# A fixed order at the head of a decoder layer, wider root tiles and other k-cuts of its input projection

## The chip, the cores and the metric

The kernel runs on one core of a Trainium2 chip. The metric is the device time of one execution in microseconds (us). Before the change it is 1656.35 us, the median of three runs (1655.63 to 1658.23). Five engines of the core work side by side, each on its own queue of instructions: TensorE (PE, matmuls; its weight loads are a row of their own, PEld), VectorE (DVE), ScalarE (ACT), GpSimd (POOL) and SyncE (SP), which here only issues DMAs.

## What is computed

One inference step of a decoder layer, for 256 new prompt tokens and 8 x 4 sample tokens, so 288 token columns (T) of 2048 features, and 9 conditioning vectors (one of the prompt, eight of the samples). In short:

```
mod  = silu(c) @ w_ada + b_ada                    # 6 x 2048 values for each vector
h    = rms(x, g_mix) * (1 + sc_m) + sh_m          # D_MODEL = 2048
proj = h @ w_in                                   # 9216 columns = 72 tiles of 128
b_gate, c_gate, hc, u, v, ga, gb = split(proj)
ya   = b_gate * shortconv(c_gate * hc);  yb = gelu(u) * spatial_gate(rms(gelu(v), g_v))
x   += gt_m * ((sigmoid(ga) * (ya @ w_pa) + sigmoid(gb) * (yb @ w_pb)) @ w_out)
h2   = rms(x, g_ffn) * (1 + sc_f) + sh_f
x   += gt_f * ((silu(gate) * up) @ w_ffn_out),   gate, up = split(h2 @ w_ffn_in)
```

The outputs are the final normalised x of both groups, the convolution states and the normalised v rows.

## The kernel before, in words

**Products.** Features lie on the partitions, tokens on the columns. Every weight matrix is streamed from memory in blocks into a ring of five raw buffers (`RAW`, 128 x 2048 float32, 1 MB, each). A block is used in pieces of at most four 128 x 128 tiles (`SEG`): ScalarE casts the piece to a rounded part `hi` (L364), VectorE subtracts it from the raw weights to get `lo` (L366); rings of four pieces each (`SPB`) hold the results. Activations are split alike. TensorE then does three matmuls of 288 columns for each weight tile: hi by hi (L380), hi by lo (L381), lo by hi (L382), into one of four PSUM banks named `pm`.

**The k-cuts of w_in.** `STREAMS` cuts the 16 feature tiles (k) of `h @ w_in`: `wA` takes k = 0 for all 72 output tiles, 8 output tiles a block (9 blocks); `wB` takes k = 1 and 2, 8 tiles a block (9 blocks); `wC` k = 3 to 7, 3 tiles a block (24 blocks); `wD` k = 8 to 15. After each pass of an output tile a "sink" moves its PSUM bank into a partial sum in SBUF: `sinkA` copies (odd tiles on ScalarE, L510, even ones on VectorE, L512), `sinkB` and `sinkC` add on VectorE (L517, L520, L523).

**The root.** The mean square of x is not known when wA begins. For the first `RAWX` = 40 tiles, wA therefore multiplies x times its gain without the root, with ten extra columns (298 in all) that carry the shift; `rescale` on GpSimd later multiplies each such partial sum by the root `rb` (L483) and adds a shift to the sample columns (L484). The squares of x are made by ScalarE and GpSimd, `sums1` adds them on TensorE, `rstd1` and `norm1` make `rb`. `mk_h1(k)` makes the normalised, modulated and split feature tile k (VectorE L203, ScalarE L233 and L239, GpSimd L236 and L237, VectorE L244).

**Modulation.** The `Ada` units aA to aE are 1 MB blocks (aA 512 KB) of `w_ada`, streamed through the same raw ring, multiplied by TensorE with the conditioning vectors as weights (L305); a `tail` (L321 to L334) brings the result into `mod`, and `gain1` makes `gm` (L492).

**What sets the order.** `steps` is a list written by hand. Up to the end of k = 7 TensorE follows it strictly (`in_order`). ScalarE and VectorE do not: a scheduler lays out their instructions, with a few explicit `behind(...)`. The loads are issued by SyncE in the order of the list, five steps ahead, each waiting for its raw buffer. While the first loads come in, `warm` matmuls on ones (L218) keep TensorE busy. `mod` of k = 0 comes from aA, of k = 1 and 2 (and 17, 18) from aB, and so on, in the order of need.

Of the kernel before, what the change touches and what calls it, by code (L numbers as in the profile page):

```python
# [12 lines left out]
P = 128  # L13
# [11 lines left out]
SPB = 4  # L25
RAWX = 40
GK = 0.7978845608028654
# [21 lines left out]
    "wA": (0, 1, 8),  # L49
    "wB": (1, 2, 8),  # L50
    "wC": (3, 5, 3),
    "wD": (8, 8, 2),
# [26 lines left out]
def _body(tc, nc, d, pc, pw, pslot, ptmp, pps):  # L79
# [20 lines left out]

    V, A, G, PE, SY = nc.vector, nc.scalar, nc.gpsimd, nc.tensor, nc.sync

# [117 lines left out]
    def scaled(k, gm, columns):  # L220
        a = tmp(TU)
        A.activation(a[:, :TP], x[:, k, :TP], AF.Copy, scale=gm[:, k, 0:1])
        G.tensor_tensor(sam(a[:, TP:T]), sam(x[:, k, TP:]), bc4(gm[:, k, 1:]), ALU.mult)  # L223
        columns(a[:, T : T + NC])
        G.memset(a[:, T + NC :], 0.0)
        return split(a, TU)

    def modulate(ks, get, gm, sh0, out):
# [112 lines left out]
    class Blk(Step):  # L341
        def __init__(self, name, idx, rhs, sink, n=T):
            self.name, self.idx, self.rhs, self.sink, self.n = name, idx, rhs, sink, n
            self.k0, self.nk, self.nm = STREAMS[name]

        def load(self):
            n = self.nk * self.nm * 128
            self.raw = pw.tile([P, n], F32, tag="raw", name=nm("raw"), bufs=RAW, padded_shape=[P, 2048])
            SY.dma_start(self.raw, d[self.name][self.idx])

        def split(self, most=99):
            n = self.nk * self.nm
            nseg = -(-n // SEG)
            per = -(-n // nseg)
            self.parts = self.parts or []
            for s in range(len(self.parts), n, per):
                if most == 0:
                    return
                most -= 1
                e = min(n, s + per)  # L360
                w = (e - s) * 128
                hi = pw.tile([P, w], F32R, tag="hi", name=nm("hi"), bufs=SPB, padded_shape=[P, SEG * 128])
                with behind(self.after if s >= self.lead else None):
                    A.copy(hi, self.raw[:, s * 128 : e * 128])  # L364
                lo = pw.tile([P, w], F32R, tag="lo", name=nm("lo"), bufs=SPB, padded_shape=[P, SEG * 128])
                V.tensor_tensor(lo, self.raw[:, s * 128 : e * 128], hi.bitcast(F32), ALU.subtract)  # L366
                for i in range(e - s):
                    self.parts.append((hi[:, i * 128 : i * 128 + 128], lo[:, i * 128 : i * 128 + 128]))

        def run(self):  # L370
            cuts = [0, self.nk] if self.name != "wD" or self.idx != 16 else [0, 5, self.nk]
            acc = {}
            for a, b, j in [(a, b, j) for a, b in zip(cuts, cuts[1:]) for j in range(self.nm)]:
                ps = acc[j] if a else acc.setdefault(j, psmain())
                for k in range(a, b):
                    wh, wl = self.parts[j * self.nk + k]
                    ah, al = self.rhs(self.k0 + k)
                    first, last = k == 0, k == self.nk - 1
                    with behind(S.get("pe")):
                        PE.matmul(ps[:, : self.n], wh, ah, start=first, stop=False)  # L380
                    PE.matmul(ps[:, : self.n], wh, al, start=False, stop=False)  # L381
                    self.last = in_order(PE.matmul(ps[:, : self.n], wl, ah, start=False, stop=last))  # L382
                if b == self.nk:
                    self.sink(self.idx * self.nm + j, ps)

# [38 lines left out]

    def squares1(k0, k1, m):
        def f():
            for k in range(k0, k1):
                q = sq[k] = slot()
                if k % 3:
                    G.tensor_tensor(q, x[:, k, :], x[:, k, :], ALU.mult)  # L430
                else:
                    with behind(evA[m]):
                        A.activation(q, x[:, k, :], AF.Square)

        return Do(f)

    def sums1():
        ps = S["sq"] = psmisc()
        for k in range(16):
            j = k % 4  # L440
            with behind(wA[2].last):
                PE.matmul(
                    ps[32 * j : 32 * j + 32, :T],
                    ones[:, :32],
                    sq.pop(k),
                    start=(k < 4),
                    stop=(k >= 12),
                    tile_position=(0, 32 * j),
                    skip_group_check=True,
                )  # L450

    def rstd1():
        q = tmp()
        A.copy(q, S["sq"][:, :T])
        r = S["r1"] = ptmp.tile([P, 3], F32, tag="r", name=nm("r"), bufs=2)
        ps = psmisc()
        for c, t0 in enumerate(TB):
            PE.matmul(ps[:, c : c + 1], q[:, t0 : t0 + P], groups, start=True, stop=True)
        V.tensor_scalar(r, ps[:, :3], 1.0 / D, EPS, ALU.mult, ALU.add)
        G.tensor_tensor(r, r, mhalf, ALU.pow)  # L460

    def norm1():
        with behind(S["pe"]):
            ps = rstd_bcast(S["r1"])
        S["rb1"] = ptmp.tile([P, T], F32, tag="rb", name=nm("rb"), bufs=1)
        A.copy(S["rb1"], ps)

    def early0():
        gain1(0, 1)

        def columns(t):
            G.tensor_copy(t, mod[:, 0, :])
            G.tensor_tensor(t[:, 1:], t[:, 1:], t[:, 0:1].to_broadcast([P, NB]), ALU.subtract)

        xe[0] = scaled(0, gm1, columns)
        wA[0].after, wA[0].lead = S["hi"], SEG

# [9 lines left out]

    xe, sq, evA = {}, {}, {}
    h1 = {}
# [16 lines left out]
    def sinkA(m, ps):  # L506
        n = TU if m < RAWX else T
        part[m] = slot(shape=(P, n))
        if m % 2:
            evA[m] = A.copy(part[m], ps[:, :n])  # L510
        else:
            V.tensor_copy(part[m], ps[:, :n])  # L512

    def sinkB(m, ps):
        a = part[m]
# [3 lines left out]
        else:  # L519
            V.tensor_tensor(a, ps[:, :T], a, ALU.add)  # L520

    def sinkC(m, ps):
        V.tensor_tensor(part[m], ps[:, :T], part[m], ALU.add)  # L523

# [223 lines left out]
    rh1 = h1.__getitem__  # L748
    aA, aB, aC, aD, aE = (ada(n) for n in ("aA", "aB", "aC", "aD", "aE"))
    wA = [Blk("wA", i, xe.__getitem__, sinkA, TU) for i in range(RAWX // 8)]  # L750
    wA += [Blk("wA", i, rh1, sinkA) for i in range(RAWX // 8, 9)]
    wB = [Blk("wB", i, rh1, sinkB) for i in range(9)]
    wC = [Blk("wC", i, rh1, sinkC) for i in range(24)]

    wA[0].defer = wA[1].defer = True
# [8 lines left out]
    steps += [Do(lambda: setattr(wA[1], "after", evA[3])), squares1(0, 6, 3), wA[1], squares1(6, 11, 9), squares1(11, 16, 15), wA[2], Do(sums1), Do(rstd1)]  # L764
# [193 lines left out]
```

## Time and profile before

| | |
|---|---|
| time, median of three runs | 1656.35 us |
| the profiled execution, its own time | 1658.97 us |
| its span in the trace | 1657.2 us |
| TensorE busy | 1632.6 us, 99% of the span |
| VectorE, ScalarE, GpSimd busy | 1004.3, 734.8, 107.6 us |
| data read | 352.56 MB, 215 GB/s over the span |
| granted TensorE clock, mean | 0.994 |

Times in the trace are counted from the span's start. A window of the trace gives the busy time of each engine in a stretch; the view of waits gives the time that an engine sat idle and what ended it; a timeline gives single instructions (start, duration), where equal neighbours are merged and counted (x4). A matmul's record is longer than its pitch, since successive matmuls overlap: the distance from start to start is what one costs.

### The profile page before, as it was taken

How to read it: one execution, taken by the hardware profiler on the slowest of the kernel's cores; microseconds unless marked ns; L12 is line 12 of the kernel's file. 1: busy time of each engine (PE TensorE's matmuls, PEld its weight loads, DVE VectorE, ACT ScalarE, POOL GpSimd, SP SyncE). 2: the span in 40 equal slices, each digit the busy share in tenths (PEclk: the TensorE clock that was granted, in tenths of full speed). 3: DMA queues.
4: the chain of work that ended last, by engine and by line, in shares of the span. 5: the costliest groups of instructions: out<-in, count | busy, mean ns of one | idle time of the engine just before them, and what ended most of it. 6: DMA issues, size and time to landing. Idle time of an engine off the chain costs nothing.

```text
span 1657.2 us, 31369 instructions
## 1 busy us (share of the span) xinstructions
PE 1632.6 (99%) x12522; PEld 1561.6 (94%) x12522; DVE 1004.3 (61%) x2036; ACT 734.8 (44%) x1364; POOL 107.6 (6%) x238
## 2 busy tenths in 40 slices
PE   8899999999999999999999999999999999999997
PEld 7789889999898999999998999999999999999997
DVE  5887557877755557557844455555555555555565
ACT  4434335643444434446733344444444444344453
POOL 3730001010100000002300000000000000000000
PEclk9999999999999999999999999999999999999998
DMA  8775776566777776664466745453455444645342
GB/s 334 283 273 174 313 292 233 189 244 255 286 308 278 282 272 254 253 256 162 150 254 252 311 159 204 162 170 130 160 203 172 160 146 155 202 159 171 125 171 75
DMA packets 56611, 357.68 MB, mean 216 GB/s; under 512 B 6432, under 2 KB 8896, under 8 KB 23312
## 3 DMA queue, kind: packets, MB, share of 16 engines
q1 hardware_dynamic: 56112, 354.95, 58.8%
q8 instruction: 98, 1.61, 0.4%
q0 software_dynamic: 352, 0.73, 0.1%
q14 instruction: 49, 0.40, 0.1%
HBM read 352.56 MB, written 3.09 MB: 215 GB/s over the span
## 4 chain that ended last, share of the span: by engine, by line
issue 50%; DVE 0%; ACT 0%; PE 0%; POOL 0%; POOLq 0%; DVEq 0%
DVE x L730 0%; PE px L183 0%; ACT t L233 0%; POOLq L944 0%; POOL t L236 0%; ACT hi L364 0%; ACT s L239 0%; DVEq L944 0%; POOL t L237 0%
## 5 line engine op out<-in xcount | busy, mean ns | idle before, releaser
L380 PE MATMUL pm<-s,hi 128*128 128x288 f32 (+1 forms) x3712 | 1101.5, 297 | 5.5 <-ACT s L510 2.7
L382 PE MATMUL pm<-s,lo 128*128 128x288 f32 (+1 forms) x3712 | 1094.8, 295 | 3.6 <-DVE lo L366 3.6
L381 PE MATMUL pm<-s,hi 128*128 128x288 f32 (+1 forms) x3712 | 1096.8, 295 | 0.9 <-DVE s L198 0.9
L364 ACT CAST hi<-raw 128x512 fp32r<-128x512 f32 (+1 forms) x966 | 581.8, 610 | 789.4 <-PE pm L381 643.7
L366 DVE TENSOR_TENSOR lo<-raw,hi 128x512 fp32r<-128x512 f32 (+1 forms) x966 | 658.3, 688 | 450.9 <-ACT hi L364 439.2
L380 PEld LDWEIGHTS pm<-s,hi 128*128 128x128 f32 x3712 | 698.7, 188 | 26.1 <-issue 15.8
L382 PEld LDWEIGHTS pm<-s,lo 128*128 128x128 f32 x3712 | 699.0, 188 | 4.4 <-DVE lo L366 4.3
L381 PEld LDWEIGHTS pm<-s,hi 128*128 128x128 f32 x3712 | 699.1, 188 | 1.1 <-DVE s L198 1.1
L305 PE MATMUL ada<-raw,cs 128*32 128x512 f32 (+2 forms) x960 | 90.5, 515 | 1.5 <-DVE cs L142 1.5
L305 PEld LDWEIGHTS ada<-raw,cs 128*32 128x32 f32 x960 | 28.3, 111 | 45.9 <-issue 39.5
L177 POOL TENSOR_TENSOR r<-r,mhalf 128x3 f32<-128x3 f32 x3 | 3.0, 990 | 863.5 <-DVE r L176 863.5
L523 DVE TENSOR_TENSOR s<-pm,s 128x288 f32<-128x288 f32 x72 | 32.8, 455 | 36.6 <-PE pm L382 36.6
L531 DVE TENSOR_TENSOR s<-pm,s 128x288 f32<-128x288 f32 x72 | 32.8, 455 | 27.3 <-PE pm L382 27.3
L196 ACT CAST s<-t 128x288 fp32r<-128x288 f32 (+1 forms) x77 | 33.3, 433 | 16.6 <-DVE t L563 7.1
L198 DVE TENSOR_TENSOR s<-t,s 128x288 fp32r<-128x288 f32 (+1 forms) x77 | 35.8, 465 | 7.3 <-ACT s L196 7.3
L260 DVE SCALAR_TENSOR_TENSOR x<-pm,mod,x 128x256 f32<-128x256 f32 x80 | 38.0, 475 | 0.0
L702 DVE SCALAR_TENSOR_TENSOR t<-t,pm 128x288 f32<-128x288 f32 x42 | 19.1, 454 | 25.3 <-PE pm L382 25.3
L483 POOL TENSOR_TENSOR s<-s,rb 128x288 f32<-128x288 f32 x40 | 33.9, 850 | 0.0
L259 DVE TENSOR_TENSOR t<-pm,mod 128x32 f32<-128x32 f32 x80 | 15.4, 192 | 29.3 <-PE pm L382 29.2
L223 POOL TENSOR_TENSOR t<-x,gm 128x32 f32<-128x32 f32 x17 | 7.6, 449 | 323.5 <-DVE gm L667 278.1
L236 POOL TENSOR_TENSOR t<-s,gm 128x32 f32<-128x32 f32 x32 | 13.4, 420 | 215.8 <-DVE gm L492 121.1
L233 ACT ACTIVATE t<-s,mod,gm 128x256 f32<-128x256 f32 x32 | 18.7, 599 | 9.8 <-DVE s L203 8.7
(131 smaller groups left out, 582.2 us busy)
## 6 DMA issues: line engine op xcount, KB each, us to landing
raw<-in_fi SPq DMA_DIRECT2D x84, 1024.0 KB, 4.9
raw<-in_a SPq DMA_DIRECT2D x64, 1024.0 KB, 6.4
raw<-in_f SPq DMA_DIRECT2D x64, 704.0 KB, 4.0
raw<-in_wD SPq DMA_DIRECT2D x36, 1024.0 KB, 5.0
raw<-in_wC SPq DMA_DIRECT2D x24, 960.0 KB, 5.9
raw<-in_aE SPq DMA_DIRECT2D x16, 1024.0 KB, 8.4
raw<-in_wo SPq DMA_DIRECT2D x16, 1024.0 KB, 7.6
raw<-in_wB SPq DMA_DIRECT2D x9, 1024.0 KB, 5.0
```

Source lines behind the costliest of these rows:

```text
L196: S["hi"] = A.copy(hi, a)
L198: S["lo"] = V.tensor_tensor(lo, a, hi.bitcast(F32), ALU.subtract)
L260: V.scalar_tensor_tensor(x[:, m, :TP], ps[:, :TP], mod[:, gt0 + m, 0:1], x[:, m, :TP], ALU.mult, ALU.add)
L305: PE.matmul(acc[32 * j : 32 * j + 32, :w], cs[:, kt, :], self.raw[:, o : o + w], start=(kt < ks), stop=(kt >= 16 - ks), tile_position=(0, ...
L364: A.copy(hi, self.raw[:, s * 128 : e * 128])
L366: V.tensor_tensor(lo, self.raw[:, s * 128 : e * 128], hi.bitcast(F32), ALU.subtract)
L380: PE.matmul(ps[:, : self.n], wh, ah, start=first, stop=False)
L381: PE.matmul(ps[:, : self.n], wh, al, start=False, stop=False)
L382: self.last = in_order(PE.matmul(ps[:, : self.n], wl, ah, start=False, stop=last))
L483: G.tensor_tensor(a[:, :T], a[:, :T], S["rb1"], ALU.mult)
L523: V.tensor_tensor(part[m], ps[:, :T], part[m], ALU.add)
L531: V.tensor_tensor(a, ps[:, :T], a, ALU.add)
```

## The change

It does seven things.

1. `RAWX` goes from 40 to 48: wA0 to wA5 run without the root, and 48 tiles are rescaled.
2. The k-cuts: the first 48 output tiles go from wA (k = 0) straight to a pass over k = 1 to 7 (`wC`, 2 tiles, 14 weight tiles a block, 24 blocks). The other 24 tiles take k = 1 to 3 (`wB`, 4 tiles, 12 weight tiles, 6 blocks) and k = 4 to 7 (`wE`, 4 tiles, 16 weight tiles, 6 blocks). 48 tiles thus have one sink less.
3. The modulation blocks: aB carries three feature tiles (k = 1, 2, 3) in eight blocks of 768 KB instead of four of 1 MB, aC the next four, aD is gone.
4. `Pinned`: each ScalarE and VectorE instruction is put behind the one before it in written order, until `free()` just ahead of wB. Casts, subtractions, squares and the making of h1 are hung at named tiles of the running wA block (`at(...)`).
5. The start: aA1 to aA3 are loaded ahead of `cp1`; wA0 comes in two loads; x of k = 0 is scaled on VectorE; `FirstBlk` runs wA0 in groups of four tiles, term by term; the warm matmuls are other counts; two later loads of x stand one block later.
6. `rescale` moves from beside wA6 to wB to the end of wB and beside wC; `mk_h1(1..3)` is spread over wA6 to wA8, `mk_h1(4..7)` stands in wB3 to wB5.
7. The first block of wD is cut at its sixth k-tile instead of its fifth.

The core of the diff:

```diff
-RAWX = 40
+RAWX = 48
-    ("aB", (17, 17, 1, 1), 2, 4),
-    ("aC", (19, 21, 3, 5), 2, 2),
-    ("aD", (23, 23, 7, 7), 1, 8),
+    ("aB", (17, 17, 1, 1), 3, 2),
+    ("aC", (20, 22, 4, 6), 2, 2),
-    "wB": (1, 2, 8),
-    "wC": (3, 5, 3),
+    "wB": (1, 3, 4),
+    "wC": (1, 7, 2),
+    "wE": (4, 4, 4),
...
+    class Pinned:
+        def __getattr__(self, name):
+            f = getattr(self.eng, name)
+            def call(*args, **kw):
+                with behind(self.last):
+                    i = f(*args, **kw)
+                if self.on:
+                    self.last = i
+                return i
+            return call
...
-    V, A, G, PE, SY = nc.vector, nc.scalar, nc.gpsimd, nc.tensor, nc.sync
+    V, A, G, PE, SY = Pinned(nc.vector), Pinned(nc.scalar), nc.gpsimd, nc.tensor, nc.sync
...
+    class FirstBlk(Blk):
+        def run(self):
+            ah, al = self.rhs(0)
+            g = SEG
+            for m0 in range(0, self.nm, g):
+                pss = [psmain() for _ in range(g)]
+                for n in range(3):
+                    for i, ps in enumerate(pss):
+                        wh, wl = self.parts[m0 + i]
+                        w, a = ((wh, ah), (wl, ah), (wh, al))[n]
...
+                for i, ps in enumerate(pss):
+                    self.sinks(m0 + i, ps)
...
     def early0():
+        a = S["x0"] = tmp(TU)
         gain1(0, 1)
...
+        V.tensor_scalar(a[:, :TP], x[:, 0, :TP], gm1[:, 0, 0:1], None, ALU.mult)
+        V.tensor_tensor(sam(a[:, TP:T]), sam(x[:, 0, TP:]), bc4(gm1[:, 0, 1:]), ALU.mult)
...
+    for b, c in zip(wA, wA[1:]):
+        at(b, j1=[c.high], j2=[c.low], j5=[c.high], j6=[c.low])
+        c.defer = True
...
+    at(wA[4], j0=[sums1_out], j2=[rstd1])
...
-    steps = [Do(silu), Do(lambda: warm(6))]
-    for s in aA:
-        steps += [s, Do(lambda s=s: warm(2, s.last))]
-    steps += [Do(early0), Do(lambda: warm(6, aA[3].last)), wA[0]]
...
-    steps += [wA[3], Do(norm1), mk_h1(0, 1)] + aB[:2] + [wA[4], wA[5]] + aB[2:] + [rescale(0, 7)]
-    steps += [gain(1, 3), wA[6], mk_h1(1, 2), wA[7], mk_h1(2, 3), rescale(7, RAWX), wA[8]]
-    steps += wB[:1] + aC[:4] + wB[1:3] + aC[4:] + [gain(3, 7)] + wB[3:4] + [mk_h1(3, 4)]
...
+    steps = [Do(silu), Do(lambda: warm(17)), *aA[:2], Do(lambda: warm(3, aA[1].last)), aA[2]]
+    steps += [Do(lambda: warm(2, aA[2].last)), aA[3], Do(lambda: warm(1, aA[3].last)), Do(aA[3].tail), Do(early0)]
+    steps += [Do(lambda: warm(4, aA[3].last))] + wA[:4] + [Do(sums1), wA[4], Do(norm1)] + aB[:4] + [Do(h1_0), wA[5]]
+    steps += aB[4:] + [Do(norms)] + wA[6:] + [Do(free), wB[0]] + aC[:4] + wB[1:3] + aC[4:]
+    steps += [wB[3], gain(4, 8), mk_h1(4, 5), mk_h1(5, 6), wB[4], mk_h1(6, 7), mk_h1(7, 8), rescale(0, 8), wB[5]]
+    steps += [rescale(8, RAWX)] + weave(wC, visits(aE, 4, gain(8, 16)), 1, 13)[:-6]
```

How instructions move at three places. In the changed kernel every ScalarE and VectorE instruction of the program carries one line, L113 (the wrapper).

**ScalarE beside wA5.** In both kernels `s` are copies of wA5's odd tiles out of `pm`; the casts make `hi` of wA6, whose raw buffer is raw_142 before and raw_161 after. Before:

```order
L510 COPY s_147_552<-pm_146_548 128x298
L510 COPY s_151_564<-pm_150_560 128x298
L364 CAST hi_161_594<-raw_142_530 128x512
L510 COPY s_155_576<-pm_154_572 128x298
L364 CAST hi_163_598<-raw_142_530 128x512
L510 COPY s_159_588<-pm_158_584 128x298
```

After:

```order
L113 ACTIVATE t_158_593<-s_157_591,mod_89,gm1_90 128x256
L113 CAST s_159_597<-t_158_593 128x288
L113 COPY s_165_613<-pm_164_609 128x298
L113 CAST hi_166_615<-raw_161_601 128x512
L113 COPY s_171_629<-pm_170_625 128x298
L113 COPY s_175_641<-pm_174_637 128x298
L113 CAST hi_176_643<-raw_161_601 128x512
L113 COPY s_181_657<-pm_180_653 128x298
```

The first cast of wA6 stood behind the copy of wA5's tile 3 and now stands ahead of it, behind that of tile 1.

**SyncE around aB.** The loads from aB's first block on; `cp` holds the second group of constants, among them the convolution state. Before:

```order
L289 DMA raw_14_160<-in_aB 128x2048
L289 DMA raw_22_197<-in_aB 128x2048
L349 DMA raw_49_267<-in_wA 128x1024
L349 DMA raw_84_353<-in_wA 128x1024
L289 DMA raw_109_437<-in_aB 128x2048
L289 DMA raw_136_511<-in_aB 128x2048
L124 DMA cp_72<-in_cpack2 128x472
L125 DMA masks_74<-in_cpack2 32x32
L349 DMA raw_142_530<-in_wA 128x1024
```

After:

```order
L328 DMA raw_50_278<-in_aB 128x1536
L143 DMA cp_72<-in_cpack2 128x472
L328 DMA raw_73_340<-in_aB 128x1536
L144 DMA masks_74<-in_cpack2 32x32
L328 DMA raw_99_408<-in_aB 128x1536
L394 DMA raw_126_493<-in_wA 128x1024
L328 DMA raw_152_566<-in_aB 128x1536
L328 DMA raw_154_573<-in_aB 128x1536
L328 DMA raw_155_579<-in_aB 128x1536
L328 DMA raw_156_585<-in_aB 128x1536
L394 DMA raw_161_601<-in_wA 128x1024
```

`cp` stood behind aB's last block and now stands behind its second; four blocks of aB now stand between wA5 (raw_84 before, raw_126 now) and wA6 (raw_142, now raw_161).

**VectorE at the copies of the state.** `zs` are two small tiles that take the convolution state out of `cp`; the `lo` rows split weights of wA. Before, behind the making of h1 of k = 0, beside wA4's first tiles:

```order
L366 TENSOR_TENSOR lo_140_519<-raw_84_353,hi_139_517 128x512
L203 TENSOR_TENSOR s_132_501<-x_75,rb_131_499 128x288
L244 TENSOR_TENSOR s_135_509<-t_133_503,s_134_507 128x288
L552 COPY zs_970_4713<-cp_72 128x8x2
L552 COPY zs_976_4758<-cp_72 128x8x2
L512 COPY s_145_546<-pm_144_542 128x298
```

After, beside wA2's last tiles:

```order
L113 COPY s_89_382<-pm_88_378 128x298
L113 COPY s_94_396<-pm_93_392 128x298
L113 COPY zs_935_4635<-cp_72 128x8x2
L113 COPY zs_941_4680<-cp_72 128x8x2
L113 TENSOR_TENSOR lo_95_398<-raw_11_155,hi_92_390 128x512
L113 COPY s_101_414<-pm_100_410 128x298
```

The two copies moved ahead of the second piece of wA3 (`lo_95`) and of all that follows it on VectorE.

## Rows read from the trace of the kernel before

**Rows 1.** Windows: length; busy us (count) of PE, PEld, DVE, ACT, POOL; PEclk, DMA, GB/s.

```profile
12.36:100.00 87.64, 77.09 (x653) 66.31 (x653) 67.19 (x121) 41.06 (x92) 59.35 (x102) 0.96 0.81 314
...
112.00:1643.00 1531.00, 1531.00 (x11628) 1473.82 (x11627) 918.00 (x1871) 686.37 (x1258) 46.22 (x123) 1.00 0.58 210
```

**Rows 2.** Waits of TensorE from 0 to 112 us; total us, times, longest us.

```profile
PE pm L382 <- DVE lo L366: 3.6, 3, 2.9
PE pm L380 <- ACT s L510: 2.7, 3, 1.4
PE pm L380 <- DVE s L517: 2.0, 2, 1.6
...
PE pm L381 <- DVE s L198: 0.9, 1, 0.9
PE px L325 <- ACT ev L321: 0.5, 1, 0.5
PE pm L380 <- DVE s L512: 0.5, 1, 0.5
```

**Rows 3.** Timeline at the start of wA0 (start us, duration us).

```profile
11.09 0.64 PE L305 MATMUL ada<-raw,cs 128*32 128x128 f32 x16
11.80 0.27 ACT L321 COPY ev<-ada 128x128 f32<-128x128 f32 x1 [6.94 <-PE ada L305]
...
13.89 0.44 ACT L196 CAST s<-t 128x298 fp32r<-128x298 f32 x1
...
14.38 0.40 PE L380 MATMUL pm<-s,hi 128*128 128x298 f32 x1
```

**Rows 4.** Timeline of TensorE in wB3, after aC's last block.

```profile
93.64 0.61 PE L382 MATMUL pm<-s,lo 128*128 128x288 f32 x1 [2.86 <-DVE lo L366]
94.05 0.44 PE L380 MATMUL pm<-s,hi 128*128 128x288 f32 x1
94.29 0.44 PE L381 MATMUL pm<-s,hi 128*128 128x288 f32 x1
...
98.93 0.29 PE L380 MATMUL pm<-s,hi 128*128 128x288 f32 x1
99.06 0.29 PE L381 MATMUL pm<-s,hi 128*128 128x288 f32 x1
```

**Rows 5.** DMA view, 14 to 62 us: GB/s in 40 slices, of 1.2 us each.

```profile
GB/s 402 420 407 410 452 430 423 430 396 416 324 331 430 48 157 403 361 148 10 184 413 379 314 27 75 266 430 341 410 423 430 423 416 430 437 294 20 0 0 0
```

**Rows 6.** Single issues, at 16.7 and 35.9 us: KB, us from issue to landing.

```profile
raw<-in_aB SPq DMA_DIRECT2D x1, 1024.0 KB, 9.3
...
raw<-in_wA SPq DMA_DIRECT2D x1, 512.0 KB, 3.4
```

**Rows 7.** Timelines of VectorE and TensorE around 35 to 38 us.

```profile
35.14 0.69 DVE L366 TENSOR_TENSOR lo<-raw,hi 128x512 fp32r<-128x512 f32 x1 [0.33 <-ACT hi L364]
...
37.85 0.86 DVE L552 COPY zs<-cp 128x16 f32<-128x16 f32 x2
...
35.19 1.93 PE L305 MATMUL ada<-raw,cs 128*32 128x256 f32 x32
```

**Rows 8.** Window of L366 alone beside `rescale`: length, then VectorE busy (instructions).

```profile
66.80:81.50 14.70, 11.40 (x8) 1.00 0.91 355
```

**Rows 9.** Timelines of VectorE and GpSimd beside `rescale`.

```profile
70.53 0.80 POOL L483 TENSOR_TENSOR s<-s,rb 128x288 f32<-128x288 f32 x1
...
75.91 1.17 DVE L366 TENSOR_TENSOR lo<-raw,hi 128x512 fp32r<-128x512 f32 x1
...
79.27 0.68 DVE L366 TENSOR_TENSOR lo<-raw,hi 128x512 fp32r<-128x512 f32 x1
...
90.56 2.33 DVE L492 SCALAR_TENSOR_TENSOR gm<-mod,cp 128x36 f32<-128x36 f32 x1
```

**Rows 10.** Sinks of VectorE on the page: busy us, mean ns, idle before.

```profile
L523 DVE TENSOR_TENSOR s<-pm,s 128x288 f32<-128x288 f32 x72 | 32.8, 455 | 36.6 <-PE pm L382 36.6
```

More of the change, by code (lines that the diff above doesn't have):

```diff
@@ L204, in normed @@
         return t
-    def behind(i):
-        return tc.issue_after(i.ins) if i is not None else ExitStack()
     def in_order(i):
@@ L344, in __init__ @@
             self.k0, self.nk, self.nm = STREAMS[name]
[L346 to L351, printed above, removed]
-            n = self.nk * self.nm
[L353 to L368, printed above, removed]
@@ new lines, in __init__, with load @@
+            n = self.nk * self.nm
+            self.per = -(-n // -(-n // SEG))
+            self.segs = [(s, min(n, s + self.per)) for s in range(0, n, self.per)]
+            self.his, self.parts, self.then = [], [], {}
+        def load(self, at=0, n=None):
+            size = self.nk * self.nm * 128
+            if at == 0:
+                self.raw = pw.tile([P, size], F32, tag="raw", name=nm("raw"), bufs=RAW, padded_shape=[P, 2048])
+            a, b = at * 128, (size if n is None else (at + n) * 128)
+            SY.dma_start(self.raw[:, a:b], d[self.name][self.idx][:, a:b])
@@ new lines, in high, with low @@
+        def high(self):
+            s, e = self.segs[len(self.his)]
+            hi = pw.tile([P, (e - s) * 128], F32R, tag="hi", name=nm("hi"), bufs=SPB, padded_shape=[P, SEG * 128])
+            self.cast = A.copy(hi, self.raw[:, s * 128 : e * 128])
+            self.his.append(hi)
+        def low(self):
+            i = len(self.parts) // self.per
+            (s, e), hi = self.segs[i], self.his[i]
+            lo = pw.tile([P, (e - s) * 128], F32R, tag="lo", name=nm("lo"), bufs=SPB, padded_shape=[P, SEG * 128])
+            V.tensor_tensor(lo, self.raw[:, s * 128 : e * 128], hi.bitcast(F32), ALU.subtract)
+            for i in range(e - s):
+                self.parts.append((hi[:, i * 128 : i * 128 + 128], lo[:, i * 128 : i * 128 + 128]))
@@ L370, in run, with split, sinks @@
+        def split(self):
+            while len(self.his) < len(self.segs):
+                self.high()
+                self.low()
+        def sinks(self, j, ps):
+            self.sink(self.idx * self.nm + j, ps)
+            for f in self.then.get(j, ()):
+                f()
         def run(self):
-            cuts = [0, self.nk] if self.name != "wD" or self.idx != 16 else [0, 5, self.nk]
+            cuts = [0, self.nk] if self.name != "wD" or self.idx != 16 else [0, 6, self.nk]
             acc = {}
@@ L423, in _body, with square @@
     S = {"strict": True}
[L425 to L435, printed above, removed]
+    def square(k, eng):
+        q = sq[k] = slot()
+        if eng is A:
+            A.activation(q, x[:, k, :], AF.Square)
+        else:
+            G.tensor_tensor(q, x[:, k, :], x[:, k, :], ALU.mult)
     def sums1():
         ps = S["sq"] = psmisc()
[L439 to L442, printed above, removed]
+        with behind(S["pe"]):
+            for k in range(16):
+                j = k % 4
+                i = PE.matmul(
                     ps[32 * j : 32 * j + 32, :T],
```

130 lines of the change are left out of this document (98 added, 32 removed).

## The prediction

> **What bounds the kernel now.** I read the windows first: which engine is full in which stretch. From 112 to 1643 us TensorE is busy in all of 1531.00 us, at a granted clock of 1.00; but of the 87.64 us from 12.36 to 100 us it is busy 77.09 [rows 1]. So 10.6 us are idle at the head, and nothing that the change does to VectorE or ScalarE behind 112 us can shorten a stretch in which TensorE never waits. Then the waits of TensorE: in that head it waits for a VectorE split (3.6 us in 3 waits), for ScalarE's copies of PSUM (2.7 in 3), for VectorE's adds (2.0 in 2) and three times for 0.5 to 0.9 us [rows 2]: 11 waits in all, each for another engine and none for a DMA. Third the timeline of TensorE: behind the longest wait, 2.86 us, the matmuls start 0.24 us apart instead of 0.13 [rows 4], so at the lower of the clock's two levels (1.2 against 2.4 GHz); from 94.05 to 98.93 us that is 21 starts in 4.88 us where 2.73 would do, 2.2 us lost.
>
> From start to start a wait costs more than its idle time: the record of 0.29 us laps 0.16 over the next start, and the first matmul behind takes 0.11 longer, so some 0.27. The head's loss between 12.4 and 100 us is therefore 10.6 idle + 2.2 slow clock + 11 x 0.27 = 3.0 for the restarts: **15.8 us, and that is all the change can win there**, beside what it makes of the first 14.4 us.
>
> **The change part by part.** I cost the head by walking through it in the new order, since nearly every edit acts there.
>
> *The sinks and k-cuts* (item 2). 48 sinks of 0.455 us on VectorE go, 22 us; but VectorE is busy 918 of the 1531 us and its sinks wait for TensorE (36.6 us before 72 of them), not TensorE for them [rows 1, 10]. Worth nothing. The number of main matmuls stays, and 8 more tiles with ten more columns, 24 matmuls, cost about 0.1 us. The bigger weight counts in a block (14 for 15, 12 and 16 for 16) keep the same bytes. The first wD block's cut (item 7) only shifts when one h1 is needed, inside a stretch without waits: nothing. aB and aD were 64 + 64 matmuls, of 256 and 128 columns; aB is now 64 of 384: some 0.2 us less.
>
> *The start* (item 5). Now aA's last matmuls start at 11.09 and end at 11.73, and the first of wA0 comes at 14.38, 2.65 us later, through the copy at 11.80 and the cast at 13.89 [rows 3]. Putting `cp1` behind aA's loads and the scaling on VectorE shortens it: aA's end about 10.9, chain 2.2, first matmul 13.1: 1.3 us won. Bounds: aA can end from 9.6 (loads as fast as the queue) to 12.6 (the warm matmuls, now 17 at first, are in its way), so from 2.6 won to 0.4 lost. `FirstBlk` asks for the split of x eight matmuls later, which removes the 0.9 us wait of L381 for `s` [rows 2]; it is among the 15.8.
>
> *wA0 to wA3 in a fixed order* (item 4). Casts and splits now fall between the copies of one wA block, where VectorE has four copies of some 0.45 and two splits of 0.69 us [rows 7, 10] for 24 matmuls at 0.14: 3.2 of 3.3 us. So close that small waits stay: I take 1.0 us for the four blocks (0 to 2).
>
> *The state's copies* (new wait). VectorE now does `zs` ahead of wA3's second split. They need `cp`, which in SyncE's order follows aB's second block. Before, aB's second block was issued at 16.70 us and landed 9.3 us later, at 26.0 [rows 6], by which time the queue had carried 8.9 MB; with wA4 and `cp` in front and two smaller aB blocks it is 9.1 MB, so `cp` lands near 26.6. Two copies of 0.43, a split of 0.69 and a copy of PSUM of some 0.5 follow [rows 7]; TensorE would want that bank 28 tiles of 0.416 us after 13.1, plus the 1.0 above, at 26; it gets it near 28.3. **2.3 us**, from 0 (if wA3 is late for another reason) to 3.
>
> *The root* comes in wA4; its chain on VectorE stands behind wA5's split, which waits for wA5's load: I take 0.9 us (0 to 2).
>
> *aB and wA6* (item 3). This is the largest term. In SyncE's order four 768 KB blocks of aB now stand between wA5 and wA6. The first may be issued early, but each of the others, and wA6, needs the raw buffer of one of aB0 to aB3, so they are issued when TensorE reaches these, at a time T. The queue moves at most 430 GB/s [rows 5]: 1.83 us for 768 KB, and a lone 512 KB takes 3.4 us [rows 6], so a lone 768 KB some 4. aB's blocks then land near T+4, 5.9, 7.7 and 9.5, wA6 near T+10.7. TensorE does aB0 to aB3 in about 2.6 us (32 matmuls of 256 columns take 1.93 [rows 7]; these have 384) and would be at wA5's tile 7 at T+5.8. Tile 7 needs the bank of tile 3, whose copy on ScalarE now stands behind the cast of wA6, which waits for the load. So TensorE stands until T+11.7: **5.9 us**, from 3 (loads at once) to 7. Behind an idle time twice the 2.86 us of [rows 4] I expect the lower clock again, 2.3 us (0 to 2.5). The waits that were here (ScalarE's copies, 2.7 us) are among the 15.8.
>
> *aC* in wB: the stall before aC's second half was 0.5 us, that behind it 2.9 [rows 2, 4]; without GpSimd's work there, and with the gain after wB3, I take 1.7 (0.5 to 3).
>
> *Rescale beside wC* (item 6). A split takes 0.69 us alone [rows 7]; beside `rescale` eight of them took 11.40, 1.42 in the mean [rows 8], single ones 1.17 and 0.68, and a tiny `gm` 2.33 us [rows 9]. So the two engines hold each other up. A wC block gives VectorE three splits of 512 columns, one of 256 and two sinks per 42 matmuls, 5.54 us: 2.07 + 0.42 + 1.04 = 3.5 us alone; with half of the 0.80 us of GpSimd's multiply [rows 9] as the mean wait, 5.1; at those eight splits' mean, 1.42, it needs 6.5. So with about ten blocks beside `rescale` the cost lies between 0 and ten times 1.0 less a lead of some three pieces (4.7 us), 5.3. I take 1.0, since the single splits behind a sink, as they stand here, were near 0.9. The Trainium skill (SBUF — State Buffer, section "Who interferes with whom") has a rule for this: a VectorE instruction with two inputs in SBUF and a GpSimd instruction that reads SBUF exclude each other for whole instructions. The trace agrees: 0.68 against 1.17 us for the same split. By it a wait is at most one GpSimd instruction, 0.8 us, a block at most 6.7 us, and with all at that end the term would be 7 us in place of 1.0 and the time 1660; the `gm` that took 2.33 us goes beyond even that.
>
> **The sum.** 1.3 (start) + 15.8 (old waits) + 0.1 (aB less the columns) - 1.0 - 2.3 - 0.9 - 5.9 - 2.3 - 1.7 - 1.0 = **2.1 us won**. Against the profiled execution's own 1658.97 us (span 1657.2) that is 1656.9; that execution stands 2.6 us above the median 1656.35, which becomes **1654.2**.
>
> **The rivals.**
> *The new load waits are short* (faster). For it: TensorE's longest waits of now all come from VectorE and ScalarE, whose order is made fixed, and no wait in [rows 2] is for a load. If wA6 lands by T+8, since its buffer comes free sooner or the queue is emptier than I think, the wait is at its low end of 3 and the clock stays up: 2.1 + 2.9 + 2.3 = 7.3 won, **1649**.
> *VectorE becomes the bound beside rescale* (slower). Place: wC, from the end of wB on, about ten blocks. Price: 5.3 us in place of 1.0, and one fall of the clock, 2.5: 2.1 - 4.3 - 2.5 = 4.7 lost, **1661.1**. It decides when a split takes over 1.2 us in the mean there (3 x 1.2 + 0.9 + 1.04 = 5.54). For: 1.42 in [rows 8]. Against: there the splits came in a row after aC, while here sinks stand between.
> *The loads set the head* (nothing changes). The DMA queue moves over 400 GB/s in most slices from 14 to 30 us [rows 5]; if the head is as long as its bytes, which the change leaves nearly alone, waits only change their names: **1656.4**. For: each new wait above is for a load. Against: after 30 us the queue drops to 10 to 48 GB/s at times [rows 5], and TensorE waits for others.
>
> **How the numbers follow.** Forecast 0.42 (1651.5 to 1657), short waits 0.23, VectorE bound 0.18, loads 0.17. A measurement of this kernel tells some 0.2%, 3.3 us, from no change: 1653.0 to 1659.7. Faster: 0.23 + 0.13 of the forecast = 0.36. Slower: 0.16 of the third, 0.03 of the rest = 0.19. Same: 0.45. The range leaves out the outer part of both rivals: 1648 to 1661.
>
> **What would show it.** In the profile of the changed kernel: TensorE waits at two places for ScalarE's or VectorE's copy of a bank where that engine itself waits for a DMA, near 26 and near 43 to 49 us, the second about 6 us long with starts 0.24 us apart behind it; first wA matmul at 13.1; splits beside `rescale` near 1 us in the mean and no wait of TensorE above 0.5 us in wC; from about 135 us on no wait at all. I am wrong if the second wait is under 3 us, if splits in wC are over 1.2 us, or if TensorE waits behind 135 us.

## The result, and the profile after

The changed kernel takes 1660.38 us, the median of 18 runs (1658.48 to 1661.57), the kernel before 1657.05 us on the same chip (18 runs, 1655.23 to 1659.81): a ratio of 1.0018, 95% interval 1.0011 to 1.0026. It is 3.3 us slower, where 2.1 us faster was forecast. The profiled execution has a span of 1659.2 us and took 1661.07 us.

First the windows of the changed kernel, in the columns of [rows 1]:

```profile
12.36:100.00 87.64, 75.01 (x621) 62.00 (x621) 50.46 (x114) 40.21 (x94) 11.66 (x23) 0.94 0.82 319
...
112.00:1643.00 1531.00, 1530.82 (x11618) 1473.37 (x11617) 917.75 (x1840) 684.83 (x1259) 100.02 (x207) 1.00 0.58 210
```

Behind 112 us TensorE is full again, beside all the `rescale` work on GpSimd (100.02 us busy there instead of 46.22), and the 48 sinks that are gone show nowhere. The head lost: 12.6 us idle instead of 10.6, at a mean granted clock of 0.94 instead of 0.96. In slices of the head:

```profile
32.00:42.00 10.00, 8.60 (x74) 6.21 (x73) 4.10 (x10) 4.20 (x10) 1.34 (x3) 1.00 0.43 135
42.00:60.00 18.00, 10.70 (x79) 7.40 (x78) 5.94 (x16) 4.41 (x11) 0.00 (x0) 0.81 0.71 266
...
80.00:100.00 20.00, 17.87 (x156) 15.24 (x155) 10.48 (x27) 5.89 (x12) 1.40 (x4) 0.91 1.00 412
```

The last two numbers are the DMA engines' share and GB/s. From 32 to 42 us the queue is at 0.43; in the slice behind it TensorE is busy in 10.70 us of 18, at 0.81 of its clock; from 80 to 100 us the queue is full at 412 GB/s. The waits of TensorE from 0 to 300 us (to be held against [rows 2]), without those under 0.6 us:

```profile
PE pm L430 <- ACT s L113: 8.0, 2, 7.3
PE ada L344 <- DMA raw<-in_aC: 1.1, 1, 1.1
PE px L234 <- DVE ones L113: 1.1, 1, 1.1
PE px L202 <- POOL r L528: 0.7, 1, 0.7
PE pm L448 <- DVE s L113: 0.6, 1, 0.6
```

The adds and splits that waited beside `rescale` before are gone from the list. One wait of 7.3 us has come, and the timelines show it as it was forecast (start us, duration us, what it waited for), first that of ScalarE:

```profile
42.27 0.41 ACT L113 COPY s<-pm 128x298 f32<-128x298 f32 x1 [1.68 <-PE pm L432]
50.55 0.62 ACT L113 CAST hi<-raw 128x512 fp32r<-128x512 f32 x1 [7.88 <-DMA raw<-in_wA]
51.08 0.71 ACT L113 COPY s<-pm 128x298 f32<-128x298 f32 x2
```

And that of TensorE:

```profile
43.94 0.29 PE L432 MATMUL pm<-s,lo 128*128 128x298 f32 x1
51.53 0.62 PE L430 MATMUL pm<-s,hi 128*128 128x298 f32 x1 [7.30 <-ACT s L113]
51.95 0.45 PE L431 MATMUL pm<-s,hi 128*128 128x298 f32 x1
52.19 0.45 PE L432 MATMUL pm<-s,lo 128*128 128x298 f32 x1
52.58 3.97 PE L344 MATMUL ada<-raw,cs 128*32 128x384 f32 x32
```

The cast of wA6 waits for its load; the copy of wA5's tile 3 stands behind it; TensorE stands in front of tile 7 and restarts at 0.24 us a matmul. A single issue, in the DMA view at 41.3 us, says when that load came (KB, us from issue to landing):

```profile
raw<-in_wA SPq DMA_DIRECT2D x1, 512.0 KB, 9.2
```

Issued when aB3's matmuls let its buffer go, it landed at 50.5 us, behind four blocks of aB.

### The profile page after: what moved, and what is told of

Its sections match the earlier page's. It is cut to its first block, busy times and chain, and to the rows that moved or that the text cites. A ratio compares the mean times of both kernels' runs of the same rounds, so it can differ in the third digit from the quotient of the medians.

```text
span 1659.2 us, 31266 instructions
## 1 busy us (share of the span) xinstructions
PE 1634.1 (98%) x12472; PEld 1562.1 (94%) x12472; DVE 986.8 (59%) x1993; ACT 734.7 (44%) x1370; POOL 120.7 (7%) x251
## 4 chain that ended last, share of the span: by engine, by line
issue 50%; DVE 0%; ACT 0%; PE 0%; POOL 0%; POOLq 0%; DVEq 0%
DVE x L113 0%; PE px L202 0%; ACT t L113 0%; POOLq L1057 0%; POOL t L275 0%; ACT hi L113 0%; ACT s L113 0%; DVEq L1057 0%; POOL t L276 0%
## 5 line engine op out<-in xcount | busy, mean ns | idle before, releaser
L113 DVE TENSOR_TENSOR lo<-raw,hi 128x512 fp32r<-128x512 f32 (+1 forms) x972 | 659.8, 686 | 481.3 <-ACT hi L113 467.6
L113 ACT CAST hi<-raw 128x512 fp32r<-128x512 f32 (+1 forms) x972 | 583.7, 607 | 797.3 <-PE pm L431 653.4
L344 PE MATMUL ada<-raw,cs 128*32 128x512 f32 (+3 forms) x896 | 90.5, 540 | 1.1 <-DMA raw<-in_aC 1.1
L113 DVE TENSOR_TENSOR s<-pm,s 128x288 f32<-128x288 f32 x120 | 54.5, 456 | 39.0 <-PE pm L432 38.7
L113 DVE TENSOR_TENSOR s<-t,s 128x288 fp32r<-128x288 f32 (+1 forms) x109 | 51.2, 471 | 12.0 <-ACT s L113 11.9
L113 ACT CAST s<-t 128x288 fp32r<-128x288 f32 (+1 forms) x109 | 47.1, 433 | 20.8 <-DVE t L113 16.4
L113 DVE SCALAR_TENSOR_TENSOR t<-t,pm 128x288 f32<-128x288 f32 x84 | 37.9, 451 | 25.2 <-PE pm L432 25.2
L562 POOL TENSOR_TENSOR s<-s,rb 128x288 f32<-128x288 f32 x48 | 43.0, 896 | 0.0
L113 DVE SCALAR_TENSOR_TENSOR x<-pm,mod,x 128x256 f32<-128x256 f32 x80 | 38.0, 476 | 0.0
L113 DVE SCALAR_TENSOR_TENSOR s<-pm,s 128x288 f32<-128x288 f32 x48 | 24.6, 512 | 15.2 <-PE pm L432 15.0
L113 DVE TENSOR_TENSOR t<-pm,mod 128x32 f32<-128x32 f32 x80 | 15.4, 192 | 29.5 <-PE pm L432 29.4
L113 DVE SCALAR_TENSOR_TENSOR s<-s,pm 128x288 f32<-128x288 f32 x32 | 14.5, 454 | 15.2 <-PE pm L432 15.2
```

Of the source, the lines that this page charges most:

```text
L113: i = f(*args, **kw)
L344: PE.matmul(acc[32 * j : 32 * j + 32, :w], cs[:, kt, :], self.raw[:, o : o + w], start=(kt < ks), stop=(kt >= 16 - ks), tile_position=(0, ...
L562: G.tensor_tensor(a[:, :T], a[:, :T], S["rb1"], ALU.mult)
```

## The experiments

Each kernel is the changed one with the edit shown, or, where the text says so, the kernel with aB spread with one more edit. The ratio is to the kernel before, run beside each; the changed kernel's is 1.0018 (1.0011 to 1.0026). Besides the ratio I read where the first block of aE starts on TensorE, in the middle of wC: it comes behind the same work in all these kernels, so it dates the end of the head. In the changed kernel that is 136.53 us. It is read from one execution, and two executions of one kernel lay 3.0 us apart in it (133.80 and 130.80, below), so differences of that size in aE alone show little.

**The casts alone.** Do the 7.3 us come from ScalarE's order or from the load?

```
-        at(b, j1=[c.high], j2=[c.low], j5=[c.high], j6=[c.low])
+        if b is wA[5]:
+            at(b, j7=[c.high, c.low, c.high, c.low])
+        else:
+            at(b, j1=[c.high], j2=[c.low], j5=[c.high], j6=[c.low])
```

> The changed kernel, but the two casts and splits of wA6 stand behind the copy of wA5's last tile on ScalarE and VectorE, so that nothing of wA5 waits for wA6's load. Theory A (wA6's load itself is late, since its raw buffer is held by aB3 until 41.2 us): TensorE finishes wA5 at about 44.4 us and does aB4 to aB7 as they land, but wA6 starts only when its load (50.5 us) is cast and split, near 52 instead of 56.5: 4 to 5 us less than the changed kernel, some 1656. Theory B (ScalarE's fixed order alone makes the wait): the 7.3 us and the slow clock behind them go altogether, 9 us less, some 1651.

Measured: 1657.29 us, ratio 1.0006 (0.9997 to 1.0016); aE starts at 133.51 us, 3.0 earlier. Theory A, though by the ratios the gain is 2 us and not 4 to 5: wA6 starts at 52.03 us, as expected. The timeline of TensorE shows the wait cut up before aB's blocks:

```profile
46.07 0.85 PE L344 MATMUL ada<-raw,cs 128*32 128x384 f32 x8 [0.29 <-DMA raw<-in_aB]
47.90 0.85 PE L344 MATMUL ada<-raw,cs 128*32 128x384 f32 x8 [0.97 <-DMA raw<-in_aB]
50.16 0.85 PE L344 MATMUL ada<-raw,cs 128*32 128x384 f32 x8 [1.41 <-DMA raw<-in_aB]
```

**One load alone.** wA6 ahead of aB4 in the order of loads.

```
+    order = list(stream)
+    order.remove(wA[6])
+    order.insert(order.index(aB[4]), wA[6])
...
-            nx = stream[i + AHEAD]
+            nx = order[i + AHEAD]
```

> The changed kernel with one load moved: wA6 ahead of aB4 to aB7 in the order of loads; all else as it is, the casts of wA6 too. Theory A: wA6 takes the buffer that is free at 38.0 us and lands near 42, so wA5 runs through without the 7.3 us wait; instead aB4 to aB7 land one behind the other up to 50 us and TensorE waits for them as matmuls; wA6 starts near 51 to 53 instead of 56.5: 4 us less, some 1656. Theory B: same kernel order on ScalarE with the load there in time, so 9 us less, some 1651.

Measured: 1657.93 us, ratio 1.0005 (0.9995 to 1.0015); aE at 131.53 us in the profiled execution, which was one of the faster ones. wA5 runs through, and TensorE waits for aB in its place: 4.0 us in 4 waits for `raw<-in_aB`, the longest 1.4. Theory A again: wA6 starts at 52.03 us here too, and whichever load stands last is late. By the ratios this gains 2 us.

**aB spread.** Take away what holds the buffers: aB0 to aB3, which hold four of the five when wA5's load takes the fifth at 30.55 us, and are used only from 38.4 us, behind sums, root and wA4. The loads on SyncE in the changed kernel:

```profile
27.75 0.34 SPq L328 DMA_DIRECT2D raw<-in_aB  x1
30.55 0.33 SPq L394 DMA_DIRECT2D raw<-in_wA  x1
37.96 3.01 SPq L328 DMA_DIRECT2D raw<-in_aB  x4
41.29 0.33 SPq L394 DMA_DIRECT2D raw<-in_wA  x1
```

From 30.55 to 37.96 us no load goes out. The edit:

```
-    steps += [...] + wA[:4] + [Do(sums1), wA[4], Do(norm1)] + aB[:4] + [Do(h1_0), wA[5]]
-    steps += aB[4:] + [Do(norms)] + wA[6:] + ...
+    steps += [...] + wA[:4] + aB[:2] + [Do(sums1), aB[2], wA[4], aB[3], Do(norm1), aB[4], Do(h1_0), wA[5]]
+    steps += aB[5:] + [Do(norms)] + wA[6:] + ...
...
+            at(b, j4=[c.high], j5=[c.low], j6=[c.high], j7=[c.low])   # wA6 in wA5
```

> The changed kernel with aB's blocks spread: aB0 and aB1 right behind wA3, aB2 ahead of wA4, aB3 behind wA4, aB4 ahead of wA5, aB5 to aB7 behind it (loads in the same order), and wA6's casts in the second half of wA5. Theory A: the four blocks of aB no longer hold four of the five raw buffers until 38.4 us, the queue is not idle from 33 to 41 us, wA6 starts near 46 instead of 56.5, and aC, whose loads follow, lands in time too: 9 to 13 us less than the changed kernel, 1647 to 1652, faster than the kernel before. Theory B: no better than the casts moved alone, or 9 us less at most through them.

Measured: 1649.06 us, ratio 0.9952 (0.9937 to 0.9967); aE at 124.55 us, 12.0 earlier. The same windows as above:

```profile
32.00:42.00 10.00, 10.00 (x93) 7.10 (x86) 3.51 (x8) 4.28 (x11) 1.34 (x3) 1.00 0.91 346
42.00:60.00 18.00, 17.67 (x135) 15.39 (x134) 15.61 (x37) 13.13 (x33) 1.91 (x6) 1.00 0.93 362
```

The queue is at 0.91 where it was at 0.43, TensorE has 10.00 of 10 and 17.67 of 18 us, and the clock stays up. Theory A, inside its range: 11 us less than the changed kernel by the ratios. The moved casts are worth some 3 us of it at most, by the first run. The loads follow the order of use, so two of them move as well: wA4's stands behind aB2's, and aB4's ahead of wA5's. The last run below takes wA4's back and keeps the gain, so the gain is not from wA4's load.

**The state's copies.** The prediction's 2.3 us.

```
-    steps.append(Do(lambda: (setattr(V, "last", None), setattr(A, "last", None))))
```

> The changed kernel, with the two copies of the convolution state kept behind the pinned part of VectorE's order, so that wA3's second split no longer waits for the second constants. The prediction put 2.3 us on that wait. If wA0 to wA3 are bound by it: wA3 ends 1.5 to 2 us earlier than at 29.55 us, wA5's load is issued as much earlier, and all behind it: 1.5 to 2.5 us less than the changed kernel, some 1658. If not (in the profile of the changed kernel TensorE waited only 0.4 us there): within 0.7 us of it, and wA3 ends between 29.0 and 29.6 us.

Measured: 1657.71 us, ratio 1.0001 (0.9992 to 1.0009), by the ratios some 3 us less than the changed kernel; aE at 133.22 us, 3.3 earlier. In the changed kernel VectorE did wait:

```profile
26.87 0.25 DVE L113 COPY zs<-cp 128x16 f32<-128x16 f32 x2 [1.20 <-DMA cp<-in_cpack]
```

TensorE hardly:

```profile
27.77 0.40 PE L432 MATMUL pm<-s,lo 128*128 128x298 f32 x1 [0.24 <-DVE lo L113]
```

Yet wA3 ends 0.9 us earlier without it (the sums start at 28.63 instead of 29.55 us), wA5's load goes out as much earlier (29.62 instead of 30.55 us) with VectorE's next split, and where wA5 starts the gain is 2.0 us (39.16 instead of 41.16). A wait of 1.2 us on an engine whose splits give buffers free costs more than TensorE shows at that place.

**rescale's place.** What does the change win by moving it?

```
-    [...] rescale(0, 8), wB[5]]
-    steps += [rescale(8, RAWX)] + weave(wC, ...
+    [...] Do(free), rescale(0, RAWX), wB[0]] + ...
+    steps += weave(wC, ...
```

> The changed kernel with all 48 rescales back in front of wB0, so that GpSimd does them beside wB and aC as in the kernel before, not beside wC. Theory C (rescale's new place is what the change gains: beside wB, where VectorE has little room, the splits waited for GpSimd; beside wC they don't): TensorE waits for splits in wB again, 4 to 9 us more than the changed kernel, 1664 to 1669. Theory D (the place does not matter, since the loads of aC and wB are the bound in that stretch anyway): within 2 us of the changed kernel, 1658 to 1662.

Measured: 1680.56 us, ratio 1.0139 (1.0126 to 1.0152), 20 us more than the changed kernel. Neither expectation: theory C's direction, but another mechanism. The timeline of ScalarE in it:

```profile
116.01 0.43 ACT L113 CAST s<-t 128x288 fp32r<-128x288 f32 x1 [21.07 <-POOL t L276]
```

And of GpSimd:

```profile
114.27 0.79 POOL L562 TENSOR_TENSOR s<-s,rb 128x288 f32<-128x288 f32 x1
...
115.42 0.24 POOL L275 TENSOR_TENSOR t<-s,gm 128x32 f32<-128x32 f32 x1
```

The small GpSimd steps of h1 of k = 4 stand behind all 48 rescales, ScalarE waits 21 us for them, and with it its casts of weights: one TensorE wait of 17.0 us. The splits that this kernel does beside `rescale` from 62 to 92 us are slower, but only by a third: 11 in 10.03 us, where the changed kernel takes 7.32 us for 11 without it. Windows of the splits alone (VectorE's busy time and count, PEclk, DMA, GB/s), of this kernel and then of the changed one:

```profile
62.00:92.00 30.00, 10.03 (x11) 1.00 0.85 340
```

```profile
62.00:92.00 30.00, 7.32 (x11) 1.00 0.90 357
```

So that place costs mostly through GpSimd's own queue, and what the new place is worth against the kernel before, where h1 was made in another order, this run doesn't say.

**The fixed order.** Without it, first alone:

```
-            self.eng, self.on, self.last = eng, True, None
+            self.eng, self.on, self.last = eng, False, None
```

> The changed kernel with the fixed order of ScalarE and VectorE taken away from the start (the scheduler places them, as in the kernel before). Theory A: wA6's load lands as late as before; depending on where the scheduler puts the casts TensorE waits in wA5 or behind aB7: 1655 to 1662. Theory B: with the fixed order the wait goes: 1653 or less.

Measured: 1651.24 us, ratio 0.9968 (0.9953 to 0.9983), against theory A, as its time goes. But aE starts at 133.80 us, where it does with the casts moved (133.51), in a profiled execution that at 1654.12 us was one of the slower ones. The rest lies where the programs have the same order of instructions: windows from 900 to 1500 us, of this kernel and of the changed one, TensorE busy throughout:

```profile
900.00:1500.00 600.00, 600.00 (x4551) 1.00 0.52 178
```

```profile
900.00:1500.00 600.00, 600.00 (x4533) 1.00 0.51 178
```

18 matmuls more in the same 600 us: 0.4%. From 300 to 900 us there is hardly a difference, 4580 against 4575. The same kernel again:

> The kernel without the fixed order of ScalarE and VectorE once more, unchanged, for the stretch behind 300 us. If its matmuls follow at 132.1 ns again from 900 to 1500 us (the changed kernel: 132.7), the pitch belongs to the program, about 3 us in all, and its lead over the changed kernel with the casts moved is not from the head. If they follow at 132.7 ns here, the pitch belongs to the single execution, and this execution's span is some 3 us longer.

Measured: 1651.52 us, ratio 0.9964 (0.9950 to 0.9979), again 4551 matmuls in that window; aE at 130.80 us. So this pitch belongs to the program, not to an execution; why is open (below). The two executions differ by 2.5 us in time and by 3.0 in aE: what differs between them lies in the head. In the changed kernel, whose loads are late, the fixed order thus costs time: without it aE comes 2.7 and 5.7 us earlier, although the first matmul of wA comes at 17.09 and 17.17 us instead of 13.99. And the fixed order taken from the kernel with aB spread:

> The kernel with aB's blocks spread, and the fixed order of ScalarE and VectorE taken away from the start. Theory A: with the loads in time the fixed order is worth little: the head within 2 us of the one with the fixed order, aE's first block at 123 to 127 us. Theory E (the run without the fixed order was faster for the order itself, not for the stretch behind 300 us, where its matmuls followed at 132.1 ns instead of 132.7): 3 to 4 us less than with aB alone spread, in the head. If the pitch behind 300 us is a matter of where the tiles lie, this run shows either pitch, whatever the head does.

Measured: 1651.60 us, ratio 0.9962 (0.9949 to 0.9975), at the usual pitch (4536 matmuls); aE at 127.32 us, 2.8 later than with the fixed order. Its loss is at the start, where the first matmul of wA comes at 16.70 us instead of 13.12: ScalarE takes two casts of wA1, which wait for their load, ahead of the cast of x.

```profile
10.99 1.14 ACT L113 CAST hi<-raw 128x512 fp32r<-128x512 f32 x2
15.17 1.14 ACT L113 CAST hi<-raw 128x512 fp32r<-128x512 f32 x2 [3.04 <-DMA raw<-in_wA]
16.21 0.44 ACT L113 CAST s<-t 128x298 fp32r<-128x298 f32 x1
```

With the loads in time the fixed order is thus a gain, of 2.8 us in the head of these two executions; the two ratios (0.9952 and 0.9962) are too close to show it in the time. It is not the order alone that made the changed kernel slow, but the order together with the late load: a cast that waits for its load then holds up the copies behind it.

**More of the same.** From the kernel with aB spread: wA5's load ahead of aB3's, the state's copies late, and aC in pieces of 2, 3 and 3 between wB0 and wB3.

```
+    order.insert(order.index(aB[3]), wA[5])
-    [Do(free), wB[0]] + aC[:4] + wB[1:3] + aC[4:]
+    [Do(free), wB[0]] + aC[:2] + wB[1:2] + aC[2:5] + wB[2:3] + aC[5:]
```

> The kernel with aB's blocks spread, and three more edits of the same kind: wA5's load ahead of aB3's, the copies of the convolution state behind the pinned part, and aC's blocks spread between wB0, wB1, wB2 and wB3 (2, 3, 3) instead of 4 and 4. Theory A (raw buffers held by modulation blocks that wait for their turn leave the queue idle): the 1.6 us wait in wA3 and about 2 us around aC's second half go: 2 to 4 us less than with aB alone spread, 1645 to 1647, ratio 0.993 to 0.994 to the kernel before. If the rest of the head is bound by the bytes of its loads instead: no better than 1649, ratio 0.995.

Measured: 1650.79 us, ratio 0.9960 (0.9947 to 0.9974); aE at 126.59 us, 2.0 later than with aB alone spread. No gain: the queue is at 0.97 from 40 to 60 us there, the wait for wA4's load in wA3 is still 1.5 us, and one for aC of 0.7 us stays. Last, from the kernel with aB spread, that one load, with the state's copies late as well:

```
+    order = list(stream)
+    order.remove(wA[4])
+    order.insert(order.index(aB[0]), wA[4])
```

> The kernel with aB's blocks spread, wA4's load ahead of aB0 to aB2, and the copies of the convolution state behind the pinned part. With aB spread TensorE still waits 1.6 us at 27.5 us for ScalarE, which waits for wA4's load (28.2 us). If the head is now bound by single late loads: wA4 lands near 22.5 us, that wait goes, and the kernel is 1 to 2 us faster than with aB alone spread, ratio 0.994 to the kernel before. If it is bound by the bytes of all its loads (the queue is at 0.9 of its share from 40 to 80 us): aB lands as much later, the wait goes elsewhere, ratio 0.995 to 0.996 as before.

Measured: 1647.63 us (1646.85 to 1648.25), ratio **0.9940** (0.9927 to 0.9952), 9.7 us under the kernel before beside it and the best of all; aE at 123.29 us. That is the expected ratio, but its interval overlaps that of aB alone spread. The loads go out here in the order of the changed kernel but for aB4, which stands ahead of wA5: most of the gain comes from when the blocks are used. Its waits on TensorE up to 112 us are all 0.6 or less but for the first ones, at the start, and its window of the head:

```profile
12.36:100.00 87.64, 84.33 (x718) 72.77 (x717) 62.41 (x135) 46.86 (x106) 20.27 (x36) 1.00 0.88 343
```

3.3 us idle in the head, against 10.6 before and 12.6 in the changed kernel.

## Why the prediction was wrong

The forecast was 5.4 us off and its direction was wrong, though the mechanism that it named as the largest term was the largest loss. The step that failed most is the price of aC, which alone takes more than the 2.1 us; three other losses came out larger than the sum had them, too. Point by point:

- **aC: the step that failed, 4.2 us for 1.7.** The 1.7 us came from the stalls before, with no fall of the clock. Around aC's second half TensorE lost 2.3 us, in waits of 1.10, 0.49 and 0.53 us and the restarts behind them, and 1.9 us behind it at the lower clock. The lost queue time from 32 to 42 us is not the reason: aC's second half is issued 11.3 us ahead of its first matmul both in the changed kernel and with aB spread (rows below), and the wait for its last block is 0.2 to 1.1 us in the kernels of this document whatever the queue did before (0.5 us with one load moved, where the queue is at 0.40 from 32 to 42 us; 0.6 in the last kernel, where it is at 0.93). The two smaller waits stand in every one of them. Of the kernels with the change, only the changed one and the one with one load moved had a mean granted clock below 1.00 from 80 to 100 us (0.91 in both). Why the wait and the clock differ between these runs is open.

```profile
74.75 2.99 SPq L328 DMA_DIRECT2D raw<-in_aC  x4
86.09 2.80 PE L344 MATMUL ada<-raw,cs 128*32 128x256 f32 x48
```

```profile
64.76 2.54 SPq L328 DMA_DIRECT2D raw<-in_aC  x4
76.10 2.80 PE L344 MATMUL ada<-raw,cs 128*32 128x256 f32 x48
```

- **aB and wA6: the mechanism right, 1.4 us too small.** The wait is 7.3 us for 5.9, with the clock's fall behind it (32 matmuls of aB took 3.97 us there, and 2.79 at 38.44 us in front of it). T came at 38.4 us; the load landed at T+12.1 instead of T+10.7. The two runs that move a cast or a load show that the load is late; the wait of ScalarE's copy on it comes from the order. The queue's best slice in [rows 5] is 452 GB/s and not 430; with that the forecast would have been earlier still.
- **The root in wA4: 2.0 us for 0.9**, two waits, both behind wA5's load (issued at 30.55 us, since its buffer also was held).
- **wA6 to wB0: 1.4 us that I had at nothing**: a wait of 0.5 us for a cast of ScalarE, which also makes three h1 in this stretch, and smaller gaps.
- **wA0 to wA3 with the state's copies: 2.3 us for 3.3.** `cp` landed just ahead of 26.87 us, forecast 26.6; TensorE came later than I thought and waited 0.24 us. The run with the copies late shows that this wait costs more behind it.
- **The start: 0.4 us won for 1.3, and it matters little.** The first matmul came at 13.99 us, but in the other kernels with this start it came between 12.47 and 13.99. With the casts moved it came at 12.47 and wA3 ended no earlier, since what ends it is the second split and the constants it waits for.
- **Rescale beside wC: right that it could be free; the 1.0 us wasn't needed.** The 29 splits of 512 columns beside it took 0.96 us in the mean, near the 1 us forecast and under the 1.2 us at which it decides:

```profile
L113 DVE TENSOR_TENSOR lo<-raw,hi 128x512 fp32r<-128x512 f32 x29 | 27.4, 955 | 12.0 <-ACT hi L113 10.5 <-PE pm L432 1.4
```

The longest was 1.35 us. This agrees with the rule in the Trainium skill (SBUF — State Buffer, "Who interferes with whom"): no split of 512 columns waited longer than one multiply of GpSimd, 0.80 us. In the kernel before, one split beside `rescale` took 3.57 us, which one such wait does not make.
- **The sinks: right.** Nothing behind 112 us changed, 4533 matmuls in 600 us for 4531 before.
- **The old waits: 15.8 was too small.** Counted over all matmuls from start to start, by my estimate, the trace of before lost 17.7 us up to 112 us, and that of after 19.4. That and the start make 1.3 us lost, and the spans differ by 2.0. The rest of the 3.3 is in the profiled executions: that of before, 1658.97 us, is 1.9 above its median of 18 runs, that of the changed kernel 0.7 above its own.

None of the three signs by which the prediction would have called itself wrong came: the second wait was not under 3 us, the splits took not over 1.2 us in the mean, and the profile has no wait of TensorE from 135 to 1640 us. They tested the mechanisms and not the sum.

The rival with VectorE as the bound gave 1661.1, nearest to the measured time, but by luck: the splits stayed under its 1.2 us. Of the mechanisms the loads that set the head came nearest, not by their bytes, as I had it, but by the buffers; that rival gave 1656.4. With aB spread, wA4's load first and the copies late the same parts are at a ratio of 0.9940, where the changed kernel is at 1.0018: some 13 us, and some 10 under the kernel before. Which parts of the change hold those 10 us is not shown, and no run spreads the modulation blocks in the kernel before.

## What to carry to other kernels

When blocks of several streams share a ring of buffers, the order in which they are used decides when the next load can go out. A group of blocks that is loaded early and used late stops the queue; look for a stretch where the DMA share falls while an engine still waits for loads further on. Moving the cast or the one load that waited won 2 us here, by the ratios; using the held blocks earlier, with the cast moved as well, won 11. Spread such groups among the blocks that free buffers quickly, and keep a cast that waits for a load behind the copies that TensorE needs.

## What was not expected of the hardware

Two programs with the same order of instructions behind 300 us keep different pitches there: 4551 against 4531 to 4536 matmuls from 900 to 1500 us, 131.8 against some 132.4 ns, in two executions of the one (the fixed order taken away) and in one each of the others. From 300 to 900 us they hardly differ (4580 against 4575 in the changed kernel). Over all that lies behind the head that is about 3 us, as much as the change itself. It isn't the free order as such, since the kernel with aB spread and a free order has the usual pitch. No run here shows the cause; it is open. A change at the head of such a kernel is better judged by when the head ends, in more than one execution, together with the total time.

The length of the waits alone does not tell when the lower clock comes. In the changed kernel three waits in a row around aC's tail, 1.10, 0.49 and 0.53 us, were followed by starts 0.24 us apart. In the kernel with one load moved they were 0.51, 0.49 and 0.53, again with starts 0.24 us apart behind them; in the kernel with wA4's load first they were 0.56, 0.49 and 0.53 at the same place, and the starts were soon 0.13 us apart. The rows of these three kernels in that order:

```profile
89.99 1.07 PE L344 MATMUL ada<-raw,cs 128*32 128x256 f32 x16 [1.10 <-DMA raw<-in_aC]
91.55 0.44 PE L364 MATMUL px<-ident,ev 128*128 128x128 f32 x2 [0.49 <-ACT ev L113]
92.52 0.59 PE L430 MATMUL pm<-s,hi 128*128 128x288 f32 x1 [0.53 <-ACT hi L113]
...
94.13 0.44 PE L432 MATMUL pm<-s,lo 128*128 128x288 f32 x1
94.37 0.44 PE L430 MATMUL pm<-s,hi 128*128 128x288 f32 x1
```

```profile
84.95 1.07 PE L344 MATMUL ada<-raw,cs 128*32 128x256 f32 x16 [0.51 <-DMA raw<-in_aC]
...
87.47 0.46 PE L430 MATMUL pm<-s,hi 128*128 128x288 f32 x1 [0.53 <-ACT hi L113]
...
89.09 0.44 PE L432 MATMUL pm<-s,lo 128*128 128x288 f32 x1
89.33 0.44 PE L430 MATMUL pm<-s,hi 128*128 128x288 f32 x1
```

```profile
77.98 1.07 PE L344 MATMUL ada<-raw,cs 128*32 128x256 f32 x16 [0.56 <-DMA raw<-in_aC]
...
80.52 0.40 PE L430 MATMUL pm<-s,hi 128*128 128x288 f32 x1 [0.53 <-ACT hi L113]
...
81.61 0.29 PE L431 MATMUL pm<-s,hi 128*128 128x288 f32 x1
81.74 0.30 PE L432 MATMUL pm<-s,lo 128*128 128x288 f32 x1
```
